# Eight state-space groups per operand set, and four weight pairs open at a feed-forward layer's start, in a hybrid encoder layer

## The chip, the cores and the metric

The kernel runs on one core of one Trainium2 chip. The metric is the time of one execution on the device in microseconds: 2114.1 us as the median of three runs (2113.96 to 2119.34).

## The reference

One encoder layer over 1024 tokens of 1024 channels, in fp32. Cut to what is computed:

```python
h = h + 0.5 * (silu(n1(h) @ Wg1) * (n1(h) @ Wu1)) @ Wd1        # n: RMSNorm, D_FF = 2816
z_ssm, q, k, v, g_ssm, g_att = split(n2(h) @ W_in)             # 512, 3 x 512, 2 x 1024 columns
# 32 groups of 16 channels, 64 complex states each, scanned in both directions
lb = exp(lam * dt);  bb = ((lb - 1) / lam) * B
s_t = lb * s_{t-1} + bb @ u_t;   y = Re(C s)                   # forward + backward, + D * z_ssm
y = gelu(y);  y = y * sigmoid(y @ W_glu + b_glu)
att = neighbourhood_attention(q, k, v)                         # 8 heads, 16 x 64 grid, window 8 x 16
h = h + (sigmoid(g_ssm) * (y @ W_bs) + sigmoid(g_att) * (att @ W_ba)) @ W_out
h = h + 0.5 * (silu(n3(h) @ Wg2) * (n3(h) @ Wu2)) @ Wd2
out = n4(h)
```

## The kernel before, in words

Every large product is made of three TensorE passes: both operands are split into a high part in the short fp32 form (`fp32r`) and the rest, and hi*hi, hi*lo, lo*hi are added up in one PSUM bank. ScalarE (ACT) makes the high part by a CAST, VectorE (DVE) the rest by a subtraction. The weights pass through the class `Weights`: SP loads a raw tile of 512 KB (`wr`, four buffers, `RAWS`), and `fill` splits up to seven units ahead into `wp` tiles.

The feed-forward layers use a scheme of seven products instead of eight for a pair of blocks. A pair f holds a row block of the gate's and one of the up projection's weights; its units q = 1 to 7 take raw quarters of them or sums of quarters (`ws`, four DVE additions per pair in `blocks`), against the matching combinations of activations in `T[q]` (tiles `tq`, split likewise). A unit is 12 matmuls of 128x512. The products of a pair share three PSUM banks, so the order of the units is free within limits: `FIRST` opens two pairs at a layer's begin, q by q; later pairs go one after the other by `THEN`. `gate_up` runs the units, takes t (ACT copy of q = 1), u and v out of PSUM, and after each unit calls `W.fill`, the deferred steps (`poke`), the steps that build further `T[q]` (`rest` in `feed`) and one piece of work put off.

The state-space layer runs in 16 blocks of two groups. Its instructions are issued by a generator, `ssm_steps`, which is advanced every sixth matmul of the gate and value products, so that TensorE goes on with those. Per block: `ssm_prep` forms the operands bb, bi, cc, ci and the padded pad (GpSimd, called POOL, does the products in `bbar`, ACT the copies); `ssm_wide` multiplies them by the tables of powers `pw` and `po` into le and lo (DVE, 128x512); `ssm_operands` makes TensorE matrices of them; `ssm_table` doubles a table of cosines and sines in seven levels, for four groups at a time; `ssm_scan` rotates, scans (four scans of 128x128) and rotates back; `ssm_leave` multiplies out. `ssm_k0`, once for every eight groups, repeats the products of `bbar` on 128x128 tiles. `ssm_params`, earlier, forms the powers and copies them into `pw` and `po` by 16 ACT copies at its end.

`project` is the product with W_out; each d and half ends in an addition to h, and in the sums of squares for the next norm: `acc` is summed over partitions by four small matmuls (ones,acc), `rstd` works on DVE from rtm to `diag`, and four matmuls by `diag` spread the result. The end of the kernel scales by the last norm in spans (`finish`, `leave`). Each engine works in its own order as written; the code's order is the schedule.

Of the kernel before, what the change touches and what calls it, by code (L numbers as in the profile page):

```python
# [43 lines left out]
RAWS, PARTS = 4, 8  # L44


FILLED, ACT, TAIL = 7, 26, 3
NP = NF // 2

FIRST = (1, 2, 6, 7, 5, 4, 3)  # L50
THEN = (1, 6, 2, 7, 5, 4, 3)


class Weights:
# [59 lines left out]
    def blocks(self, p):  # L114
# [12 lines left out]
        st["S"] = {1: a11, 6: s2, 2: a12, 7: s3, 5: a21, 4: a22, 3: s4}  # L127
        st["left"] = {0: {1, 2}, 1: {4, 5}}
# [5 lines left out]
    def prepare_one(self):  # L134
# [16 lines left out]
        else:  # L151
# [4 lines left out]
            else:  # L156
                p, q = u[1:]
                self.blocks(p)
                st = self.pairs[p]
                src = st["S"][q]  # L160
                if q == 6:
                    self.step(4)
# [7 lines left out]
            else:  # L170
                for i, left in st["left"].items():
                    if q in left:
                        left.remove(q)
                        if not left:
                            self.drop(st["raw"] + i)
# [5 lines left out]
        if u[0] == "p":  # L181
            for v in self.units[self.split : self.split + 4]:
                if v[0] == "p" and self.loaded >= self.pairs[v[1]]["raw"] + 2:
                    self.blocks(v[1])

# [23 lines left out]
class Body:  # L209
# [35 lines left out]
    def rstd(self, st, half, then=None, n=HALF, keep=True, at=0):  # L245
# [24 lines left out]
        self.defer(1, spread)  # L270
# [71 lines left out]
    def plan_ffn(self, W, name, wg, wu, wd, plain):  # L342
# [4 lines left out]
        order = [((name, f), q) for q in FIRST for f in fs[:2]] + [((name, f), q) for f in fs[2:] for q in THEN]  # L347
# [25 lines left out]
    def combine(self, x, gcol=None):  # L373
# [34 lines left out]
        g = lambda k: self.vecs[:, gcol + k : gcol + k + 1]  # L408

# [7 lines left out]
        def ahead_scaled(rs):  # L417

            for j in range(4):
                f[2].append(small())  # L420
                m(f[3][j], f[3][j], rs, ALU.mult)
                less(f[2][j], f[3][j], b11[j])
                part(6, j, f[2], 4)
            for j in range(4):
                m(b12[j], b12[j], rs, ALU.mult)
            for j in range(4):
                self.scale(x, j + 4, 1, gcol, rs)

        def diff(o, u, v):
# [10 lines left out]
            "T3": lambda: parts(7, f[3], 4),  # L440
            "t1": lambda: diff(b12, b11, b12),
# [64 lines left out]
    def gate_up(self, plain, after):  # L506
# [5 lines left out]
        order = [(f, q) for q in FIRST for f in fs[:2]] + [(f, q) for f in fs[2:] for q in THEN]  # L512
# [4 lines left out]
        for n, (f, q) in enumerate(order):  # L517
# [31 lines left out]
            elif q == 3:  # L549
# [4 lines left out]
                st[f] = None  # L554
            W.fill(FILLED)
# [37 lines left out]
    def feed_down(self, h, src, done, spans):  # L593
# [70 lines left out]
        for j, sl in enumerate(spans):  # L664
            for i in range(4):
# [5 lines left out]
                work()  # L671
# [3 lines left out]
        work(NF)  # L675


    def ssm_params(self, pool, keep):
# [119 lines left out]
        cmul(lam(5, 4), lam(1, 4), wide(4, 4), 4)  # L798
        yield
# [32 lines left out]

        self.PW, self.PO = (keep.tile([P, 2, NB, 2, 2, 8], F32, name=n) for n in ("pw", "po"))
        for c in (0, 1):
            for i in (0, 1):
                for o, x, y in (
                    (self.PW, L[0:64, c, 0:8, :], L[64:128, c, 7::-1, :]),
                    (self.PO, L[0:64, c, 1:9, :], L[64:128, c, 8:0:-1, :]),
                ):
                    for half, z in ((slice(0, 64), x), (slice(64, 128), y)):  # L840
                        nc.scalar.copy(o[half, c, :, i], z.rearrange("p s (b g) -> p b g s", g=2))
        yield

    def ssm_k0(self, q):
# [3 lines left out]
        bc = pool.tile([P, 8, 64], F32, name="k0bc", bufs=1)  # L848
# [1012 lines left out]
```

## Time and profile before

| what | value |
| --- | --- |
| median of 3 runs | 2114.1 us |
| the profiled execution | 2112.26 us, span 2110.4 us |
| mean granted TensorE clock | 0.982 |
| PE / PE weight load busy | 95% / 77% |
| DVE, ACT, POOL busy | 69%, 40%, 10% |
| DMA | 316.59 MB, 150 GB/s mean |

Times in the trace count from the span's start. The stages, roughly: feed-forward 1 to 700 us, state-space inputs to 735, gates and values with the state-space blocks to 1072, attention, gating and W_out to 1440, feed-forward 2 to the end. Matmuls overlap, so the sum of their durations says little; the steady pace is read from the number of matmuls in a stretch without a wait.

### The profile page before, as it was taken

The numbers are of one execution on the slowest core, as the hardware profiler recorded it, in microseconds if no ns is written. First come the engines' busy times: TensorE is split into PE (matmuls) and PEld (weight loads), VectorE is DVE, ScalarE is ACT, GpSimd is POOL, SyncE is SP. The second block draws the span as 40 slices with busy tenths as digits, with TensorE's granted clock in tenths as the row PEclk, the third lists the DMA queues.
The fourth block names the chain that finished last, engine by engine and source line by source line (L and its number), as shares of the span: only waits on it lengthen the run. The fifth ranks groups of instructions, "written<-read, shape, count | busy, mean of one in ns | idle before, by whom it ended". The sixth has DMA issues, their size and how long they took to land.

```text
span 2110.4 us, 26907 instructions
## 1 busy us (share of the span) xinstructions
PE 2008.1 (95%) x9394; PEld 1633.4 (77%) x9394; DVE 1455.4 (69%) x2711; ACT 834.9 (40%) x1595; POOL 221.1 (10%) x308
## 2 busy tenths in 40 slices
PE   8999999999999799899999999997999999999996
PEld 6778888878888688677877778775788888878885
DVE  6986666656566658898565778668766666657556
ACT  7332233224545324334444573334323222334443
POOL 0011101100000033342000303100001100000000
PEclk9999999999999999999999999999999999999998
DMA  4167666648655143232321333532556665457553
GB/s 175 68 170 188 182 168 175 164 155 279 230 201 189 47 142 98 91 102 89 132 78 43 98 122 123 206 124 76 149 166 181 150 190 155 141 188 273 180 193 120
DMA packets 167879, 316.59 MB, mean 150 GB/s; under 512 B 20288, under 2 KB 40384, under 8 KB 167744
## 3 DMA queue, kind: packets, MB, share of 16 engines
q1 hardware_dynamic: 148608, 288.72, 40.4%
q0 software_dynamic: 12672, 23.07, 7.5%
q10 hardware_dynamic: 6464, 3.08, 0.5%
q8 instruction: 74, 1.21, 0.2%
q14 instruction: 61, 0.50, 0.1%
HBM read 244.88 MB, written 116.10 MB: 171 GB/s over the span
## 4 chain that ended last, share of the span: by engine, by line
PE 69%; DVE 20%; ACT 5%; issue 3%; DMA 2%; ACTq 0%; POOL 0%; SPq 0%; DVEq 0%; POOLq 0%
PE ps L214 68%; DVE tq L301 1%; DVE wp L166 1%; DVE tab L937 1%; DVE wp L146 1%; DVE ww L1026 1%; DVE tb L1012 1%; DVE lt L928 1%; DVE ta L1011 1%; DVE gl L1494 1%; PE ps L1281 1%; ACT wp L145 1%; DVE le L928 1%; DMA h<-in_x 1%; DMA y<-ys 1%
## 5 line engine op out<-in xcount | busy, mean ns | idle before, releaser
L214 PE MATMUL ps<-tq,wp 128*128 128x512 f32 x3444 | 795.1, 392 | 22.1 <-DVE u L515 8.3
L214 PEld LDWEIGHTS ps<-tq,wp 128*128 128x128 f32 x3444 | 648.9, 189 | 167.7 <-DVE tq L301 10.2
L214 PE MATMUL ps<-ap,wp 128*128 128x512 f32 (+1 forms) x1884 | 426.0, 387 | 6.4 <-ACT ap L300 4.0
L214 PEld LDWEIGHTS ps<-ap,wp 128*128 128x128 f32 x1884 | 349.7, 189 | 81.2 <-ACT ap L300 5.2
L214 PE MATMUL ps<-uh,wp 128*128 128x512 f32 x1088 | 327.1, 406 | 17.3 <-ACT wp L145 17.3
L214 PEld LDWEIGHTS ps<-uh,wp 128*128 128x128 f32 x1088 | 206.4, 193 | 65.7 <-ACT wp L145 18.5
L166 DVE TENSOR_TENSOR wp<-wr,wp 128x512 fp32r<-128x512 f32 x318 | 217.5, 685 | 53.3 <-ACT wp L165 53.2
L165 ACT CAST wp<-wr 128x512 fp32r<-128x512 f32 x318 | 191.5, 616 | 61.5 <-PE ps L214 60.1
L214 PE MATMUL ps<-ul,wp 128*128 128x512 f32 x544 | 185.6, 401 | 2.0 <-DVE ul L280 2.0
L545 ACT ACTIVATE v<-v 128x512 f32<-128x512 f32 x41 | 25.9, 632 | 318.0 <-DVE v L515 318.0
L301 DVE TENSOR_TENSOR ap<-ar,ap 128x512 fp32r<-128x512 f32 x154 | 105.8, 688 | 59.6 <-ACT ap L300 59.0
L300 ACT CAST ap<-ar 128x512 fp32r<-128x512 f32 x154 | 95.4, 620 | 114.6 <-DMA ar<-tq 108.1
L146 DVE TENSOR_TENSOR wp<-wr,wp 128x1024 fp32r<-128x1024 f32 (+2 forms) x72 | 85.9, 1197 | 66.3 <-ACT wp L145 65.8
L214 PEld LDWEIGHTS ps<-ul,wp 128*128 128x128 f32 x544 | 103.7, 192 | 25.4 <-DVE ul L280 2.8
L166 DVE TENSOR_TENSOR wp<-ws,wp 128x512 fp32r<-128x512 f32 x123 | 84.1, 685 | 48.7 <-ACT wp L165 48.7
L87 POOL DMA_DIRECT2D sums<-in_wd x44 | 36.7, 925 | 599.7 <-DMA sums<-in_wd 599.7
L214 PE MATMUL ps<-m,wp 128*128 128x512 f32 x384 | 90.6, 397 | 5.2 <-ACT m L300 3.3
L515 DVE TENSOR_TENSOR v<-t,ps 128x512 f32<-128x512 f32 x41 | 28.1, 686 | 93.9 <-PE ps L214 93.9
L626 DVE SCALAR_TENSOR_TENSOR h<-ps,h 128x512 f32<-128x512 f32 (+1 forms) x76 | 48.6, 657 | 63.7 <-PE ps L214 63.7
L214 PEld LDWEIGHTS ps<-m,wp 128*128 128x128 f32 x384 | 73.0, 191 | 22.1 <-ACT m L300 3.7
L165 ACT CAST wp<-ws 128x512 fp32r<-128x512 f32 x123 | 75.2, 615 | 22.2 <-DVE ws L125 22.2
L145 ACT CAST wp<-wr 128x1024 fp32r<-128x1024 f32 (+2 forms) x72 | 71.0, 996 | 1.4 <-issue 1.3
(215 smaller groups left out, 2254.3 us busy)
## 6 DMA issues: line engine op xcount, KB each, us to landing
ar<-tq SPq DMA_DIRECT2D x154, 256.0 KB
wr<-in_wg SPq DMA_DIRECT2D x44, 512.0 KB
wr<-in_wu SPq DMA_DIRECT2D x44, 512.0 KB
sums<-in_wd SPq DMA_DIRECT2D x88, 256.0 KB
wr<-sums SPq DMA_DIRECT2D x88, 256.0 KB
wr<-in_wd SPq DMA_DIRECT2D x66, 256.0 KB
tq<-t SPq DMA_DIRECT2D x61, 256.0 KB
wr<-in_w_in SPq DMA_DIRECT2D x28, 512.0 KB
```

The source lines that it names most:

```text
L87: self.nc.gpsimd.dma_start(out=out, in_=x, accum_op=ALU.add, max_dma_last_dim=2048)
L145: nc.scalar.copy(hi[:, a:b], raw[:, a:b])
L146: nc.vector.tensor_tensor(out=lo[:, a:b], in0=raw[:, a:b], in1=hi[:, a:b].bitcast(F32), op=ALU.subtract)
L165: nc.scalar.copy(hi, src)
L166: nc.vector.tensor_tensor(out=lo, in0=src, in1=hi.bitcast(F32), op=ALU.subtract)
L214: self.nc.tensor.matmul(out, lhsT, rhs, start=start, stop=stop, skip_group_check=go_on)
L300: self.nc.scalar.copy(hi, x)
L301: self.nc.vector.tensor_tensor(out=lo, in0=x, in1=hi.bitcast(F32), op=ALU.subtract)
L515: add = lambda o, u, v: nc.vector.tensor_tensor(out=o, in0=u, in1=v, op=ALU.add)
L545: nc.scalar.activation(out=s["v"], in_=s["v"], func=AF.Silu, scale=-1.0)
L626: nc.vector.scalar_tensor_tensor(out=t, in0=bank[:, sl], scalar=c, in1=t, op0=ALU.mult, op1=ALU.add)
L928: m = lambda o, x, y, op: self.nc.vector.tensor_tensor(out=o, in0=x, in1=y, op=op)
```

## The change

Two things, with small ones beside them. (1) The state-space operands are made for eight groups at once (`ssm_quad`): products on DVE, copies on ACT, only a memset on POOL. The tables of cosines and sines are made for eight groups as well, operands and all that follows come one iteration later (21 iterations instead of 20), le and lo lie in the big pool, and lt shares a buffer with ta. The powers are copied right after they are formed, pw by ACT, po by POOL. (2) `FIRST` becomes a list of 28 units that opens four pairs. Units q = 1 and 2 read the raw tile without waiting for its sums. There are five raw buffers and 24 instead of 26 activation buffers; T2 and the rest are built in smaller steps, later; `project` fills the weights at its end and forms sums early (`early`). The deferred norm of half 1 starts one step earlier. At the start a small activation is put ahead of the loads; at the end ACT scales all spans.

```diff
-RAWS, PARTS = 4, 8
-FILLED, ACT, TAIL = 7, 26, 3
+RAWS, PARTS = 5, 8
+FILLED, ACT, TAIL = 7, 24, 3
-FIRST = (1, 2, 6, 7, 5, 4, 3)
+FIRST = tuple((int(x[1]), int(x[0])) for x in "10 11 12 20 21 22 13 60 61 23 70 71 50 51 40 41 30 31 62 72 52 42 32 63 73 53 43 33".split())
+def order_of(fs):
+
+    return [(fs[i], q) for i, q in FIRST] + [(f, q) for f in fs[4:] for q in THEN]
...
             if p not in self.pairs:
-                self.pairs[p] = {"raw": len(self.raws)}
...
+        self.steps.append(lambda: self.done(p, "sums"))
+        st["S"] = {6: s2, 7: s3, 5: a21, 4: a22, 3: s4}
+    def done(self, p, q):
+
+        st = self.pairs[p]
+        for i, left in st["left"].items():
+            if q in left:
+                left.remove(q)
+                if not left:
+                    self.drop(st["raw"] + i)
...
-                self.blocks(p)
-                st = self.pairs[p]
-                src = st["S"][q]
-                if q == 6:
-                    self.step(4)
+                if q < 3:
+                    i = self.pairs[p]["raw"]
+                    self.load(i + 1)
+                    while i not in self.tiles:
+                        self.step()
+                        self.load(i + 1)
+                    src = self.tiles[i][:, hs(q - 1)]
+                else:
+                    self.blocks(p)
+                    src = self.pairs[p]["S"][q]
+                    if q == 6:
+                        self.step(5)
...
+    def early(self, n):
+
+        ps = []
+        for u in self.units[self.split :]:
+            if u[0] != "u" and u[1] not in ps:
+                ps.append(u[1])
+            if len(ps) == 2:
+                break
+        for p in ps:
+            if self.loaded >= self.pairs[p]["raw"] + 2:
+                self.blocks(p)
+        self.step(n)
```
```diff
+            self.poke()
-        rest = {2: ("T3",), 4: ("t1",), 5: ("T1", "t4"), 7: ("T4",), 9: ("B22",)}
+        rest = {4: ("T3",), 5: ("b12",), 6: ("t1",), 7: ("T1",), 8: ("b22",), 9: ("t4",), 10: ("T4",), 12: ("B22",)}
-            self.poke()
...
+        self.PW, self.PO = (keep.tile([P, 2, NB, 2, 2, 8], F32, name=n) for n in ("pw", "po"))
+        for c in (0, 1):
+            for i in (0, 1):
+                for copy, o, x, y in (
+                    (nc.scalar.copy, self.PW, L[0:64, c, 0:8, :], L[64:128, c, 7::-1, :]),
+                    (nc.gpsimd.tensor_copy, self.PO, L[0:64, c, 1:9, :], L[64:128, c, 8:0:-1, :]),
+                ):
+                    for half, z in ((slice(0, 64), x), (slice(64, 128), y)):
+                        copy(o[half, c, :, i], z.rearrange("p s (b g) -> p b g s", g=2))
...
-        self.PW, self.PO = (keep.tile([P, 2, NB, 2, 2, 8], F32, name=n) for n in ("pw", "po"))
...
```
```diff
+        bs, cs = (pool.tile([P, 4, 3, 2, 16], F32, tag=n, name=n, bufs=2) for n in ("bs", "cs"))
+        pad = pool.tile([P, 4, 2, 2, 2, 16], F32, name="pad", bufs=2)
+        t = pool.tile([P, 4, 2, 16], F32, name="bt", bufs=1)
+        m = lambda o, x, y, op: nc.vector.tensor_tensor(out=o, in0=x, in1=y, op=op)
+        blocks = lambda x: x.rearrange("p (b g) k -> p b g k", g=2)
+        fr, fi = (blocks(self.f[:, c, gs].unsqueeze(2).to_broadcast([P, 8, 16])) for c in (0, 1))
+        br, bi, cr, ci = (blocks(bc[:, :, 16 * i : 16 * i + 16]) for i in range(4))
+        nc.gpsimd.memset(pad, 0.0)
+        for o, x, y, op in ((bs[:, :, 1], br, bi, ALU.subtract), (bs[:, :, 2], bi, br, ALU.add)):
+            m(o, x, fr, ALU.mult)
+            m(t, y, fi, ALU.mult)
+            m(o, o, t, op)
+        for o, x, sign in ((bs[:, :, 0], bs[:, :, 2], -1.0), (cs[:, :, 0], cr, 1.0), (cs[:, :, 1], ci, -1.0), (cs[:, :, 2], cr, -1.0)):
+            nc.scalar.activation(out=o, in_=x, func=AF.Copy, scale=sign)
+        for d in (0, 1):
+            s = slice(64 * d, 64 * d + 64)
+            for c in (0, 1):
+                nc.scalar.copy(pad[s, :, c, :, d, :], bs[s, :, 1 + c])
+        flat = pool.tile([P, 2, 4, 32], F32, name="flat", bufs=1)
+        for c in (0, 1):
+            nc.scalar.copy(flat[:, c], bs[:, :, 1 + c].rearrange("p b g k -> p b (g k)"))
+        self.quads[q] = (bs, cs, pad)
...
```
```diff
-        if b % 2 == 0:
-            tab = self.tab = pool.tile([P, 2, 4, P], F32, tag="tab", name="tab", bufs=1)
+        if b % 4 == 0:
+            tab = self.tab = pool.tile([P, 2, 8, P], F32, tag="tab", name="tab", bufs=1)
+            gs = slice(2 * b, 2 * b + 8)
-                sh = [P, 2, 4, n]
+                sh = [P, 2, 8, n]
-                y = pool.tile([P, 2, 4, 64], F32, tag="tb", name="ty", bufs=1)[:, :, :, 0:n]
-                m(new, old, self.cosines[:, i, g4].unsqueeze(1).unsqueeze(3).to_broadcast(sh), ALU.mult)
-                m(y, old[:, ::-1], self.sines[:, i, :, g4].unsqueeze(3).to_broadcast(sh), ALU.mult)
+                y = pool.tile([P, 2, 8, 64], F32, tag="ty", name="ty", bufs=1)[:, :, :, 0:n]
+                m(new, old, self.cosines[:, i, gs].unsqueeze(1).unsqueeze(3).to_broadcast(sh), ALU.mult)
+                m(y, old[:, ::-1], self.sines[:, i, :, gs].unsqueeze(3).to_broadcast(sh), ALU.mult)
                 m(new, new, y, ALU.add)
...
```
```diff
-        self.load_bc(0)
-        k0 = [self.ssm_k0(q) for q in range(4)]
-        next(k0[0])
-        for n in range(NB + 4):
+        for n in range(NB + 5):
             if 0 <= n - 3 < NB:
-                self.ssm_enter(n - 3)
+                self.ssm_loads(n - 3)
+            if 0 <= n - 4 < NB:
+                self.ssm_enter(n - 4)
             yield
-            scan = self.ssm_scan(n - 3) if 0 <= n - 3 < NB else iter(())
-            if 0 <= n - 4 < NB:
-                self.ssm_leave(n - 4)
+            if 0 <= n - 5 < NB:
+                self.ssm_leave(n - 5)
-            if 0 <= n - 1 < NB:
-                self.ssm_operands(n - 1)
-            if n == 1 or (n % 4 == 0 and 0 < n < NB):
-                next(k0[n // 4])
+            if 0 <= n - 2 < NB:
+                self.ssm_operands(n - 2)
+            if n == 1:
+                next(quad[0])
+            if n % 2 and n // 4 < 3:
+                next(quad[n // 4 + 1])
             yield
-            if n < NB:
-                self.ssm_prep(n)
-                self.ssm_table(n - 2)
+            if 0 <= n - 3 < NB:
+                self.ssm_table(n - 3)
+            if n == 0 or (n % 4 == 2 and n // 4 < 3):
+                next(quad[(n + 2) // 4])
...
```
```diff
+            else:
+
+                W.prepare(W.at + 3)
...
+                if half and d == KD - 1:
+                    W.fill(PARTS)
+                if half and d > 3:
+                    W.early(3)
...
+            self.eps = const.tile([P, 1], F32, name="eps")
+            nc.vector.memset(self.eps, EPS)
+
+            nc.scalar.activation(out=const.tile([P, 1], F32, name="none"), in_=self.eps, func=AF.Square)
...
@@ -1660,8 +1684,8 @@
-                steps["T2"]()
-                self.feed(steps, 3, {0: lambda: self.evac_plain(*held.pop(0)), 3: lambda: self.evac_plain(*held.pop(0))})
+                evac = lambda: self.evac_plain(*held.pop(0))
+                self.feed(steps, 3, {0: evac, 1: steps["T2"], 3: evac})
...
-                        self.defer(2, lambda: self.rstd(sums[half], half, (first, second)[half], HALF, False))
+                        self.defer(2 - half, lambda: self.rstd(sums[half], half, (first, second)[half], HALF, False, 0, 1 + half))
```
```diff
-                        if at == last:
-                            nc.vector.scalar_tensor_tensor(
-                                out=t, in0=t, scalar=self.vecs[:, GF + k : GF + k + 1], in1=rs[:, :n],
-                                op0=ALU.mult, op1=ALU.mult,
-                            )
-                        else:
-                            nc.vector.tensor_tensor(out=t, in0=t, in1=rs[:, :n], op=ALU.mult)
+                        nc.vector.tensor_tensor(out=t, in0=t, in1=rs[:, :n], op=ALU.mult)
-                        if at:
+                        if at == last:
                             leave(k)
                         else:
                             self.todo.append(lambda k=k: leave(k))
-                            if i < last:
-                                tt = h[d][half][:, spans[i][1]]
-                                nc.scalar.activation(out=tt, in_=tt, func=AF.Copy, scale=self.vecs[:, GF + d : GF + d + 1])
+                            tt = h[d][half][:, spans[i][1]]
+                            nc.scalar.activation(out=tt, in_=tt, func=AF.Copy, scale=self.vecs[:, GF + d : GF + d + 1])
...
+                self.work(KD // 2)
+                self.poke()
+                self.poke()
+                self.work(KD)
                 while self.later:
                     self.poke()
```

On ACT, where the state-space inputs are made, this is the order before (wr to wp are weight splits, `sines` and `pw`, `po` belong to `ssm_params`):

```order
L145 CAST wp<-wr 128x1024
L266 COPY rs<-ps 128x512
L831 ACTIVATE sines<-sines 128x32 x7
L841 COPY pw<-lpow 64x16x16 x2
L841 COPY po<-lpow 64x16x16 x2
L841 COPY pw<-lpow 64x16x16 x2
L841 COPY po<-lpow 64x16x16 x2
L841 COPY pw<-lpow 64x16x16 x2
L841 COPY po<-lpow 64x16x16 x2
L841 COPY pw<-lpow 64x16x16 x2
L841 COPY po<-lpow 64x16x16 x2
L145 CAST wp<-wr 128x1024 x3
```

and after:

```order
L159 CAST wp<-wr 128x1024
L849 COPY pw<-lpow 64x16x16 x8
L296 COPY rs<-ps 128x512
L882 ACTIVATE sines<-sines 128x32 x7
L159 CAST wp<-wr 128x1024 x3
L907 ACTIVATE bs<-bs 128x4x32
L907 ACTIVATE cs<-bc 128x4x32 x3
L911 COPY pad<-bs 64x4x2x16 x4
L914 COPY flat<-bs 128x128 x2
L1182 COPY g<-ps 128x512 x2
L159 CAST wp<-wr 128x1024
```

The eight pw copies have moved ahead of `rs` and the sines, the po copies have left ACT, and the three splits follow the sines directly.

On PE behind the last block's products (`sx,lo`), before; `uh`, `ul` against `wp` are the value products, and the attention starts behind them:

```order
L214 MATMUL ps<-sx,lo 128x128 x2
L214 MATMUL ps<-wp,uh 128x512 x9
L214 MATMUL ps<-wp,ul 128x512 x4
L214 MATMUL ps<-wp,uh 128x512 x4
L214 MATMUL ps<-wp,ul 128x512 x4
L214 MATMUL ps<-wp,uh 128x512 x12
L214 MATMUL ps<-wp,ul 128x512 x4
L214 MATMUL ps<-wp,uh 128x512 x4
L214 MATMUL ps<-wp,ul 128x512 x4
L214 MATMUL ps<-wp,uh 128x512 x12
L214 MATMUL ps<-wp,ul 128x512 x4
L214 MATMUL ps<-wp,uh 128x512 x4
```

(two more rows of 4 and 8 of them follow), and after:

```order
L244 MATMUL ps<-sx,lo 128x128 x2
L244 MATMUL ps<-wp,ul 128x512 x3
L244 MATMUL ps<-wp,uh 128x512 x12
L244 MATMUL ps<-wp,ul 128x512 x4
L244 MATMUL ps<-wp,uh 128x512 x4
L244 MATMUL ps<-wp,ul 128x512 x4
L244 MATMUL ps<-wp,uh 128x512 x8
L244 MATMUL ps<-uh,wp 128x512 x2
```

77 value matmuls stood behind the last block, and 35 stand there now.

On DVE at the end of W_out, before, behind the last row block's `tf` (L125 forms the sums of weights, L166 the lower parts, L239 begins the norm):

```order
L125 TENSOR_TENSOR ws<-wr 128x512
L166 TENSOR_TENSOR wp<-wr,wp 128x512 x2
L125 TENSOR_TENSOR ws<-ws,wr 128x512
L125 TENSOR_TENSOR wr<-wr 128x512
L125 TENSOR_TENSOR ws<-wr,ws 128x512
L125 TENSOR_TENSOR ws<-wr 128x512
L166 TENSOR_TENSOR wp<-ws,wp 128x512
L125 TENSOR_TENSOR ws<-ws,wr 128x512
L125 TENSOR_TENSOR wr<-wr 128x512
L125 TENSOR_TENSOR ws<-wr,ws 128x512
L166 TENSOR_TENSOR wp<-ws,wp 128x512 x3
L239 TENSOR_SCALAR rtm<-ps 128x8
```

and after, from the splits ahead of the last addition to h (L1571) on:

```order
L187 TENSOR_TENSOR wp<-wr,wp 128x512 x5
L1571 TENSOR_TENSOR h_11695<-h_11695,ps 128x512
L263 TENSOR_TENSOR acc<-acc,sq 128x512
L444 SCALAR_TENSOR_TENSOR tf<-h_11695,vecs,tf 128x512
L269 TENSOR_SCALAR rtm<-ps 128x8
L270 RECIPROCAL rt<-rtt 128x8
L271 TENSOR_TENSOR rtt<-rt 128x8
L272 SCALAR_TENSOR_TENSOR rtt<-rtt,rtm 128x8
L273 SCALAR_TENSOR_TENSOR rt<-rtt,rt 128x8
L286 TENSOR_SCALAR diag<-ident,rt 128x128 x4
```

Fourteen sums and splits have left the place between the last `tf` and the norm; five splits in a row, and three sums ahead of them, now stand before the last addition to h.

## Rows read from the trace of the kernel before

**Rows 1.** Stretches: start:end, length, busy by engine (instructions), clock, DMA share, GB/s.
```profile
50.00:100.00 50.00, 45.09 (x187) 36.42 (x186) 49.01 (x80) 19.04 (x35) 0.00 (x0) 0.94 0.20 74
100.00:150.00 50.00, 45.17 (x191) 34.92 (x190) 40.56 (x67) 19.14 (x34) 4.24 (x5) 1.00 0.52 146
700.00:740.00 40.00, 29.44 (x123) 23.91 (x122) 26.67 (x113) 14.50 (x27) 0.00 (x0) 0.87 0.27 67
845.60:971.60 126.00, 113.89 (x601) 94.04 (x600) 109.24 (x246) 48.36 (x126) 49.10 (x88) 0.96 0.30 93
1400.00:1450.00 50.00, 42.69 (x178) 33.20 (x176) 40.00 (x68) 21.23 (x35) 0.00 (x0) 0.97 0.27 92
1450.00:1510.00 60.00, 48.94 (x190) 36.44 (x191) 50.84 (x83) 23.71 (x41) 5.03 (x6) 0.94 0.44 124
1600.00:1650.00 50.00, 50.00 (x223) 41.40 (x222) 33.76 (x54) 15.40 (x28) 6.03 (x8) 1.00 0.61 162
```
**Rows 2.** PE's waits by line and releaser: us in total, times, longest.
```profile
PE ps L214 <- ACT wp L145: 18.9, 4, 10.6
PE ps L214 <- POOL bt L878: 8.8, 7, 1.5
PE ps L214 <- DVE u L515: 8.3, 4, 2.7
PE ps L214 <- DVE diag L256: 7.4, 4, 4.4
PE ps L960 <- DVE le L928: 7.3, 5, 2.0
PE ps L214 <- ACT qk L1214: 4.4, 1, 4.4
```
**Rows 3.** Time lines of PE and of SP's queue, start of feed-forward 1.
```profile
80.98 5.38 PE L214 MATMUL ps<-tq,wp 128*128 128x512 f32 x23
91.60 0.33 SPq L105 DMA_DIRECT2D wr<-in_wg  x1
```
**Rows 4.** Time line of ACT at the state-space inputs: start, us, instruction, count.
```profile
720.64 1.27 ACT L841 COPY pw<-lpow 64x256 f32<-64x256 f32 x2
...
730.75 2.94 ACT L145 CAST wp<-wr 128x1024 fp32r<-128x1024 f32 x3
```
**Rows 5.** DVE groups, 845.6 to 971.6 us: busy us, mean ns, idle before.
```profile
L1026 DVE TENSOR_TENSOR_SCAN ww<-rho,ww 128x128 f32<-128x128 f32 x32 | 12.4, 447 | 0.0
L937 DVE TENSOR_TENSOR tab<-tab,ty 128x8 f32<-128x8 f32 (+6 forms) x28 | 8.7, 312 | 1.0
L937 DVE TENSOR_TENSOR tab<-tab,cosines 128x8 f32<-128x8 f32 (+6 forms) x28 | 8.7, 311 | 1.0
L146 DVE TENSOR_TENSOR wp<-wr,wp 128x1024 fp32r<-128x1024 f32 x7 | 8.7, 1240 | 5.2 <-ACT wp L145 5.2
L937 DVE TENSOR_TENSOR ty<-tab,sines 128x8 f32<-128x8 f32 (+6 forms) x28 | 8.5, 304 | 0.0
L928 DVE TENSOR_TENSOR lt<-pw,bi 128x512 f32<-128x512 f32 x8 | 5.5, 687 | 8.3 <-ACT bi L907 8.3
```
**Rows 6.** Time line of PE in a block: small products and the next.
```profile
858.55 0.61 PE L214 MATMUL ps<-sx,lo 128*128 128x128 f32 x4
859.00 0.39 PE L214 MATMUL ps<-su,sm 128*128 128x128 f32 x2
```
**Rows 7.** DVE, same stretch, one form of the table apart.
```profile
L937 DVE TENSOR_TENSOR tab<-tab,ty 128x128 f32<-128x128 f32 x4 | 1.2, 292 | 0.1
```
**Rows 8.** Time line of DVE: four scans beside POOL's k0 products, and without.
```profile
916.10 2.10 DVE L1026 TENSOR_TENSOR_SCAN ww<-rho,ww 128x128 f32<-128x128 f32 x4
930.71 1.36 DVE L1026 TENSOR_TENSOR_SCAN ww<-rho,ww 128x128 f32<-128x128 f32 x4
```
**Rows 9.** Time lines of ACT's first instruction and of DVE's leaves in the last span but one.
```profile
4.15 1.28 ACT L279 ACT_TABLE_LOAD   x1 [4.15 <-DMA h<-in_x]
2094.03 2.77 DVE L1754 TENSOR_TENSOR h<-h,rs 128x256 f32<-128x256 f32 x8
```

More of the change, by code (lines that the diff above doesn't have):

```diff
@@ L79, in plan_pairs @@
             if p not in self.pairs:
-                self.pairs[p] = {"raw": len(self.raws)}
+                self.pairs[p] = {"raw": len(self.raws), "left": {0: {1, 2, "sums"}, 1: {4, 5}}}
                 self.raws.extend(pairs[p])
@@ L170, in prepare_one @@
             else:
[L171 to L175, printed above, removed]
+                self.done(p, q)
         if self.split in self.jobs:
@@ L182, in prepare_one @@
             for v in self.units[self.split : self.split + 4]:
-                if v[0] == "p" and self.loaded >= self.pairs[v[1]]["raw"] + 2:
+                if v[0] == "p" and v[2] > 2 and self.loaded >= self.pairs[v[1]]["raw"] + 2:
                     self.blocks(v[1])
+    def early(self, n):
[9 more added lines that the diff above has]
+        self.step(n)
     def cost(self, i):
@@ L243, in rsqrt, with rstd @@
         nc.vector.scalar_tensor_tensor(out=y, in0=t, scalar=1.5, in1=y, op0=ALU.add, op1=ALU.mult)
-    def rstd(self, st, half, then=None, n=HALF, keep=True, at=0):
+    def rstd(self, st, half, then=None, n=HALF, keep=True, at=0, wait=1):
         nc = self.nc
@@ L268, in spread @@
                 then(self.rs[half] if keep else ps)
-        self.defer(1, spread)
+        self.defer(wait, spread)
     def enter(self, h, k, half, gcol, u, pool, tag):
@@ L346, in plan_ffn @@
         fs = range(plain, NF)
-        order = [((name, f), q) for q in FIRST for f in fs[:2]] + [((name, f), q) for f in fs[2:] for q in THEN]
+        order = [((name, f), q) for f, q in order_of(fs)]
         sums = self.sums[name]
@@ L417, in ahead_scaled, with second @@
         def ahead_scaled(rs):
[L419 to L427, printed above, removed]
+            for j in range(5):
+                if j < 4:
+                    f[2].append(small())
+                    m(f[3][j], f[3][j], rs, ALU.mult)
+                    less(f[2][j], f[3][j], b11[j])
+                if j:
+                    part(6, j - 1, f[2], 4)
+            scales.append(rs)
+        def second(rows):
+            for rs in scales:
+                for j in range(4):
+                    if rows:
+                        self.scale(x, j + 4, 1, gcol, rs)
+                    else:
+                        m(b12[j], b12[j], rs, ALU.mult)
         def diff(o, u, v):
@@ L511, in gate_up @@
         fs = range(plain, NF)
-        order = [(f, q) for q in FIRST for f in fs[:2]] + [(f, q) for f in fs[2:] for q in THEN]
+        order = order_of(fs)
         st = {f: {} for f in fs}
@@ L923, in ssm_wide @@
+        st["le"] = place("le")
+        st["lo"] = place("lo")
         for o, w, x, y in ((st["le"], self.PW, bb, bi), (st["lo"], self.PO, cc, ci)):
[L924 removed]
+            t = pool.tile([P, 2, 2, 8, 16], F32, tag="ta", name="lt", bufs=1)
             f = lambda v: v.rearrange("p c g s k -> p (c g) s k")
```

97 lines of the change are left out of this document (20 added, 77 removed).

## The prediction

> **What bounds the kernel now.** The stretches of the trace come first, because a mean over the whole span mixes stages. In a steady feed-forward stretch TensorE (PE) has 223 matmuls in 50 us, no wait and full clock, so 0.224 us is the price of a 128x512 matmul (1600 to 1650) [rows 1]. VectorE (DVE) and ScalarE (ACT) are busy for 34 and 15 of those 50 us. The change alters neither the number of large matmuls nor their kind, so time can only come from stretches with fewer of them. There are four: 378 where 446 would fit (50 to 150), 123 where 179 would (700 to 740), 368 where 491 would (1400 to 1510), and the state-space blocks. Counted as matmuls of 0.224 us that is 15.2, 12.5 and 27.6 us. The waits by releaser then say on whom PE waits there: one ACT split for 10.6 us, POOL's bt and DVE's le in the blocks for 16.1, u and diag at the feed-forward begins, qk once for 4.4 [rows 2]. The clock falls beside such waits (0.94, 0.87, 0.94 in rows 1), which is why the counts lose more than the waits' sum.
>
> **Feed-forward 1, the begin.** Four pairs open instead of two, so q = 6 and later come further behind their sums. But PE reaches units faster than weights come. The first unit starts at 80.98 and a unit lasts 12 x 0.224 = 2.7 us, so the fifth, 21, is due at 91.7. The seventh, 13, needs the seventh raw tile, and with five buffers it can be asked for only when the sums of pairs 0 and 1 are done; before, SP asks for a tile of this layer at 91.60 [rows 3]. 512 KB at the 146 GB/s of the stretch from 100 to 150 are 3.6 us (an estimate), so ACT, which splits ahead in order, stands at 13's CAST until about 95, and is through with it and the next copy, 0.6 us each, some 2 us later. Behind that CAST on ACT is the copy of t for the next pair, which frees the bank for 21: I expect PE to wait there for about 5.7 us. Against that the waits for u, some others and most of the reduced clock go: of 15.2 lost I let 11.7 remain. Term: +3.5. Bounds: +10 if the raw comes in time, -2 if the clock falls beside the longer pause as it does now (0.94 from 50 to 100).
>
> **State-space inputs.** ACT works from 720.64 on 16 copies of powers and starts the next weight split at 730.75; PE waits for that split 10.6 us [rows 2, 4]. After, the pw copies stand ahead of the sines, beside matmuls that are already fed, and the po copies are on POOL, which is idle there (0.00 busy in the stretch). The split then follows the last of the sines at about 720.7. A gap of about 1 us stays, since the split and its lower part take 1.0 and 1.2 us. Of 12.5 lost 11.5 return. Bounds 9 to 12.5; if the cover of the copies is gone, they cost eight times 0.63 us, still half of before.
>
> **State-space blocks.** Between 845.6 and 971.6 there are 32 scans, so eight iterations of 15.75 us, in which DVE is busy for 109.24 / 8 = 13.65 and idle for 2.1; half of that, 8.3 / 8 = 1.04, is lt waiting for ACT's bi, which waits for POOL [rows 1 and 5]. DVE with its waits sets the period. An iteration is seven steps, one at every sixth large matmul: 42 of the 601 / 8 = 75 matmuls are large and 33 small. The next small product starts 0.45 us after four of them (858.55 to 859.00), 0.112 each [rows 6], so PE needs 9.4 + 3.7 = 13.1 us. Per iteration the change:
> - takes the wait for bi away (operands are there an iteration ahead): -1.04;
> - doubles the tables. Now one costs (8.7 + 8.7 + 8.5) / 4 = 6.5 us per two iterations [rows 5]. For eight groups every level is twice as wide: the smallest level (3 x 0.17) goes and one of 128x1024 comes, 3 x 1.24 by the split of that size. 9.7 us per four iterations against 13: -0.8;
> - adds six products of 128x128 per four iterations to DVE, 0.29 each [rows 7]: +0.45;
> - takes POOL's products away from beside DVE. Four scans take 1.36 us alone and 2.10 beside POOL's k0 products [rows 8]; all 32 took 12.4 instead of 10.9: -0.2;
> - adds lt's wait for ta's buffer, which ACT's copies of the scan free: the nearest row is the split's wait for ACT, 5.2 / 8; I take a third of it less than what otherwise goes, -0.3 for all small waits.
>
> The sum is 15.75 - 1.9 = 13.85. About 13 iterations have everything, so 24.7 us. A table for eight groups is a burst of 9.7 instead of 6.5 us, with scan and leave behind it in DVE's order; the operands stand an iteration ahead, which hides about half. I take 1.5 us of PE wait for each of three such bursts inside. Term: +20. Lower bound +8: only the wait for bi goes (13.5) and a burst costs the 3.2 us it grew, with some clock. Upper bound +31: the period is PE's 13.1 (13 x 2.65 = 34, less the bursts).
>
> On the fourth item the Trainium skill (SBUF — State Buffer, "SBUF: two separate sides") says that a DVE instruction with two inputs in SBUF and a GpSimd instruction that reads SBUF exclude each other for the whole instruction. The trace shows a lengthening, not a whole wait: 0.74 us on four scans. By the rule DVE could win back up to POOL's busy time, 49.1 / 8 = 6.1 us an iteration, and PE would set the period; that is the rival below.
>
> **Attention's begin.** PE waits 4.4 us for qk [rows 2]. The chain from the last block's leave over gelu and back is the same, but 35 value matmuls instead of 77 stand behind the last `sx,lo`, since the blocks end one iteration later: 42 x 0.224 = 9.4 us less cover. Part returns, as ACT's q copies now go between. Term: -6; bounds -9.4 and 0.
>
> **Feed-forward 2, the begin.** The norm's start, rtm, no longer has 14 sums and splits ahead of it, so most of the 4.4 us for diag goes, and T2 no longer stands in one piece before the first units; u (5.8 of its 8.3 us lie here) has more units to come in [rows 2]. In return three sums and five splits, 8 x 0.6 = 4.8 us, stand before the last addition to h, and ones,acc waits for it: I expect 5.5 us there and about 3 at T4. Of 27.6 lost 13.5 return. Bounds +22 (a rest of 5.5) and +8 (only the 4.4 and half of u's waits).
>
> **Start and end.** ACT's table load (1.28 us) begins only when h has landed at 4.15 [rows 9]; put ahead of it, up to 1.3 return, or nothing if the first weights come later still: +0.6. The Trainium skill (ScalarE: Activation LUTs, "What ACT_TABLE_LOAD costs") counts 2.7 us for a switch, with a drain; by it the term would be up to 2.7. The row has 1.28. At the end the eight products of the last span but one (2.8 us of DVE) are put off until the last sums are through [rows 9]: +2.7, bounds 2 and 4, the upper by the plain product in the last span. The down products (activation buffers 24 for 26): 0, bounds -2 and +1; DMA has 0.61 of its share there, and the loads are issued well ahead.
>
> **Sum.** 3.5 + 11.5 + 20 - 6 + 13.5 + 0.6 + 2.7 = 45.8. The profiled execution took 2112.3 us, 1.8 less than the median; 2112.3 - 45.8 + 1.8 = 2068.
>
> **Rivals.**
> - The openings give nothing: raw tiles come too late at both begins, and the 17 us stay. For: five buffers for eight raws; against: at feed-forward 2 the tiles can be loaded during W_out. 2085.
> - The bursts cost in full: blocks +8, and qk -9.4. For: DVE has 2.1 us of slack per iteration and a burst of 9.7; against: operands an iteration ahead. 2068 + 12 + 3.4 = 2083. With the first: 2100.
> - PE sets the period, as when POOL's products cost DVE more than the scans show: +31 in the blocks, and feed-forward 2 nearer its bound: 2048. Against: DVE would still be busy for 13.1 us.
> - Slower: activation buffers run out at the begins. Four open pairs hold t, u, v, twelve of 24 tiles, where two held six of 26, beside T's own tiles. Then DVE's next sum waits, behind it all splits, until a pair closes; a pair is seven units, 19 us. Twice 19 against 28.8 of gains elsewhere (45.8 - 17): 2123. It decides from 14 us a begin. Against: pairs 0 and 1 close before 2 and 3 take u and v.
> - It doesn't do what it says: another engine sets every stretch, 2114.
>
> **Chances.** Forecast 0.41, openings 0.17, bursts 0.14, both 0.07, PE-bound 0.07, slower 0.08, nothing 0.06. The range 2046 to 2102 leaves out the last two. Within 0.3% (6.3 us, what a measurement here can tell) lies the last, 0.06; slower 0.08; faster 0.86.
>
> **What would show it.** In the changed profile: no wait of more than 2 us for wp at 720 to 735; blocks about 13.9 us apart with no wait for bi, POOL nearly idle; a longer wait for qk; 1400 to 1510 with about 430 large matmuls instead of 368; at 80 to 150 one wait of 5 to 6 us for t. The forecast is wrong if the blocks stay above 15 us, or if waits for activation tiles appear on DVE at the begins.

## The result, and the profile after

The changed kernel takes 2126.45 us as the median of six runs (2126.22 to 2128.23), against 2115.7 us for the kernel before in its six runs: the ratio is 1.0052, with a 95% interval of 1.0041 to 1.0062. The change makes the kernel half a per cent slower; the forecast was 2068 us and the range ended at 2102. The profiled executions lie 15.1 us apart (spans 2110.4 and 2125.5), as that of before (2112.26 us) was faster than each of its six timed runs.

The profile after, PE's waits by line and releaser (us in total, times, longest), in answer to [rows 2]:

```profile
PE ps L244 <- DVE u L555: 19.8, 5, 8.8
PE ps L244 <- ACT wp L159: 12.1, 4, 6.1
PE ps L244 <- DMA su<-zs: 10.6, 2, 7.6
PE ps L244 <- ACT qk L1232: 10.6, 1, 10.6
PE ps L244 <- ACT sx L1056: 9.9, 3, 4.9
PE ps L244 <- DVE acc L263: 8.9, 3, 5.3
PE ps L244 <- ACT t L576: 6.3, 1, 6.3
```

What was to go has gone: bt and le are no releasers any more, diag has 3.4 us left, and the ACT split's longest wait is 6.1 us, at the kernel's start. In their place stand new ones: u rose from 8.3 to 19.8, qk from 4.4 to 10.6, and su and sx are new. All of PE's waits together rose from 95.3 to 107.0. In stretches (busy us and instructions by engine, clock, DMA share, GB/s), in answer to [rows 1]:

```profile
100.00:150.00 50.00, 43.32 (x183) 35.42 (x183) 45.71 (x75) 23.90 (x44) 4.18 (x5) 0.94 0.42 115
700.00:740.00 40.00, 33.23 (x131) 26.24 (x130) 32.47 (x162) 10.11 (x19) 4.99 (x8) 0.92 0.19 41
809.30:1021.00 211.70, 191.25 (x1012) 160.57 (x1013) 167.90 (x338) 80.29 (x154) 1.05 (x2) 0.95 0.28 93
1465.00:1545.00 80.00, 67.91 (x274) 52.77 (x273) 64.33 (x104) 29.07 (x52) 4.13 (x5) 0.91 0.35 96
```

The begins of the two feed-forward layers (first and last row) still run at a granted clock of 0.94 and 0.91. The third row holds 14 iterations of the blocks, from first scan to first scan. DVE is busy for 167.90 / 14 = 12.0 us in each, less than the 13.1 that were forecast, and yet an iteration lasts 15.1 us. In the kernel before the same 14 iterations are

```profile
790.10:1004.40 214.30, 197.31 (x1039) 162.94 (x1038) 186.92 (x424) 84.41 (x213) 75.59 (x132) 0.96 0.30 94
```

15.3 us each, with DVE at 13.35 and PE at 14.1. DVE lost a tenth of its work and the period one per cent.

**The blocks.** The longest wait there, by engines, in the changed kernel (start, us, engine, line, what; the wait in brackets). First DVE: it ends a table for eight groups, then forms the next le and lo, and only then splits a weight. Then SP's queue, then PE:

```profile
927.48 1.23 DVE L954 TENSOR_TENSOR tab<-tab,ty 128x1024 f32<-128x1024 f32 x1
...
932.48 1.22 DVE L160 TENSOR_TENSOR wp<-wr,wp 128x1024 fp32r<-128x1024 f32 x1
933.62 0.69 DVE L1028 TENSOR_TENSOR ta<-ev,tab 128x512 f32<-128x512 f32 x1
```

```profile
933.73 0.33 SPq L110 DMA_DIRECT2D wr<-in_w_v  x1
934.15 0.38 SPq L1001 DMA_DIRECT2D su<-zs  x1
```

```profile
937.68 1.62 PE L244 MATMUL ps<-su,let 128*128 128x128 f32 x6 [7.62 <-DMA su<-zs]
```

The releaser named is a DMA, but it was only issued at 934.15: SP works in order, the weight load ahead of it waits for a raw buffer, and that comes free when DVE is through with the split at 933.7, 14.6 us after the table began. At the other tables PE waits 3.03 (su), 4.51 and 4.87 us (both sx), 20.0 us at the four together.

**The begins of the feed-forward layers.** DVE at the first of them, the three additions to u (L555), and PE's waits:

```profile
139.56 0.68 DVE L555 TENSOR_TENSOR u<-u,ps 128x512 f32<-128x512 f32 x1
143.29 0.68 DVE L555 TENSOR_TENSOR u<-u,ps 128x512 f32<-128x512 f32 x1
147.02 0.68 DVE L555 TENSOR_TENSOR u<-t,ps 128x512 f32<-128x512 f32 x1
```

```profile
98.66 1.65 PE L244 MATMUL ps<-tq,wp 128*128 128x512 f32 x3 [6.30 <-ACT t L576]
147.84 2.47 PE L244 MATMUL ps<-tq,wp 128*128 128x512 f32 x5 [6.68 <-DVE u L555]
166.01 2.40 PE L244 MATMUL ps<-tq,wp 128*128 128x512 f32 x6 [1.88 <-DVE u L555]
```

The first two additions close pairs 0 and 1 (units 30 and 31), and each is followed on DVE by two products, sums for the down layer and weight splits. The third is that of unit 62, ready at 147.7, which unit 72 needs. Counted by the k-th unit of the layer, the changed kernel is 7 us ahead at the 18th unit, and 6 behind after the 26th. In the second layer, counted from its first unit, it makes up 13.9 us until the 18th and loses 14.7 in the next eight (a wait of 8.77 for u).

**The state-space inputs.** ACT, DVE and PE:

```profile
717.45 5.17 ACT L849 COPY pw<-lpow 64x256 f32<-64x256 f32 x8 [22.61 <-DVE lpow L733]
722.65 0.59 ACT L296 COPY rs<-ps 128x512 f32<-128x512 f32 x1
731.16 0.23 ACT L882 ACTIVATE sines<-sines 128x32 f32<-128x32 f32 x1 [7.93 <-DVE sines L739]
```

```profile
723.27 3.16 DVE L1142 TENSOR_TENSOR z<-ps,rs 128x512 f32<-128x512 f32 x3 [3.22 <-ACT rs L296]
```

```profile
720.11 0.79 PE L244 MATMUL ps<-uh,wp 128*128 128x512 f32 x1 [3.44 <-DVE z L1142]
735.71 0.73 PE L244 MATMUL ps<-uh,wp 128*128 128x512 f32 x2 [3.33 <-ACT wp L159]
```

The eight copies now hold up rs, rs holds up z on DVE, z the sines, and the split that follows the last of these starts at 734.63, not at 720.7. The copies could not start earlier: ACT stood idle for 22.61 us until DVE had powers to copy. DVE's chain that forms them begins late, for it waits for its parameters (sraw). SP's queue, then DVE:

```profile
686.25 10.97 SPq L110 DMA_DIRECT2D wr<-in_w_in  x3
697.32 0.38 SPq L723 DMA_DIRECT2D sraw<-in_ssm_p  x1
```

```profile
700.51 0.18 DVE L741 TENSOR_SCALAR sp<-sraw 128x32 f32<-128x32 f32 x1 [3.64 <-DMA sraw<-in_ssm_p]
```

The early third weight split has brought a third weight load in front of sraw. That load went out only at 696.90, when DVE was through with the split and a raw buffer came free, and sraw behind it. In the kernel before SP issues sraw at 681.79, and DVE begins on it at 689.63 without a wait.

**Attention's begin**, in answer to the 4.4 us of [rows 2]:

```profile
1091.15 1.31 PE L244 MATMUL ps<-qk 64*128 64x256 f32 x6 [10.59 <-ACT qk L1232]
```

### The profile page after: what moved, and what is told of

Read it like the earlier page. It is cut to its first block, busy times and chain, and to the rows that moved or that the text cites. A ratio compares the mean times of both kernels' runs of the same rounds, so it can differ in the third digit from the quotient of the medians.

```text
span 2125.5 us, 26603 instructions
## 1 busy us (share of the span) xinstructions
PE 2012.1 (95%) x9394; PEld 1642.3 (77%) x9394; DVE 1446.1 (68%) x2643; ACT 834.7 (39%) x1540; POOL 134.3 (6%) x144
## 4 chain that ended last, share of the span: by engine, by line
PE 71%; DVE 18%; ACT 4%; DMA 3%; issue 3%; SPq 0%; ACTq 0%; DVEq 0%
PE ps L244 71%; DVE tq L331 1%; DVE tab L954 1%; DVE wp L187 1%; DVE wp L160 1%; ACT wp L159 1%; DVE gl L1512 1%; PE ps L1299 1%; DMA h<-in_x 1%; DVE ty L954 1%; DMA y<-ys 0%; DVE ww L1043 0%; DVE ws L130 0%; DVE u L555 0%; DVE ta L1028 0%
## 5 line engine op out<-in xcount | busy, mean ns | idle before, releaser
L244 PE MATMUL ps<-tq,wp 128*128 128x512 f32 x3444 | 795.8, 393 | 26.9 <-DVE u L555 19.8
L555 DVE TENSOR_TENSOR v<-t,ps 128x512 f32<-128x512 f32 x41 | 28.2, 687 | 83.3 <-PE ps L244 83.3
```

Source lines behind the costliest of these rows:

```text
L244: self.nc.tensor.matmul(out, lhsT, rhs, start=start, stop=stop, skip_group_check=go_on)
L555: add = lambda o, u, v: nc.vector.tensor_tensor(out=o, in0=u, in1=v, op=ALU.add)
```

## The experiments

Differences in us are ratios to the kernel before, times its 2115.7; the changed kernel is at +11.0. The block stage is counted from PE's first gate product to its wait for qk: 340.2 us in the kernel before, 344.8 in the changed one.

**e1, the state-space part alone, and e2, the rest alone.** The diff in two: `ssm_params` to `ssm_inputs` in e1, all else in e2; for e1, against the changed kernel, among others

```diff
-RAWS, PARTS = 5, 8
-FILLED, ACT, TAIL = 7, 24, 3
+RAWS, PARTS = 4, 8
+FILLED, ACT, TAIL = 7, 26, 3
-        order = order_of(fs)
+        order = [(f, q) for q in FIRST for f in fs[:2]] + [(f, q) for f in fs[2:] for q in THEN]
```

and the reverse in e2.

> The kernel before with the state-space part of the change alone (powers copied when formed, operands and tables for eight groups, 21 iterations, early third weight split); all feed-forward, norm, start and end edits are left out. Theory, parts are independent: from the two traces the inputs gain 2.2 us, the blocks lose 4.6, the wait for qk loses 6.2, attention 0.9, so about 9.5 us slower than before, near 2125. Rival, the state-space part is good and only meets late weights of the feed-forward part: 20 us faster than before, near 2095.

> The kernel before with everything but the state-space part: four open pairs, five raw buffers, 24 activation buffers, later T steps, early sums, norm, start and end edits. Theory, independent parts: feed-forward 1 loses 6.3 us, the begin of feed-forward 2 loses 0.8, its down products 1.9, the end gains 3.2: 5.8 us slower, near 2121. Rival, the late state-space part disturbs the second feed-forward layer: no slower than before, 2112 to 2115.

Measured: 2122.86 us, ratio 1.0025 (1.0014 to 1.0037), and 2120.83, ratio 1.0022 (1.0012 to 1.0032). Each part by itself makes the kernel slower, e1 by less than expected, and 5.3 + 4.7 is about the 11.0 of both: within the intervals the parts add. The wait for sraw stands in e1's trace (3.8 us) and not in e2's.

**e3, the closings apart.**

```diff
-... 50 51 40 41 30 31 62 72 52 42 32 63 73 53 43 33
+... 50 51 40 41 30 62 31 72 52 63 42 73 32 53 43 33
```

> The changed kernel with another order of the same 28 units: 62 stands between the closing units 30 and 31, and 63, 73 between 52, 42 and 32, so that no two pairs close back to back ahead of a unit that needs its u. Theory, DVE's backlog of two closings delays u of pair 2: the waits of 6.7 and 8.8 us for u fall below 3 each and the trailing ones of 1.9 go, so 10 to 15 us less than the changed kernel, 2111 to 2116. Rival, weights or activation buffers come late there: the waits move with the units and the time stays at 2126.

Measured: 2111.41, ratio 0.998 (0.997 to 0.999), 15.2 us less than the changed kernel. All waits for u together:

```profile
PE ps L244 <- DVE u L555: 5.5, 3, 2.5
```

against 19.8. Buffers, loads and the number of open pairs are the same, so these waits were DVE's backlog behind two closings. The wait for t at unit 21 is not among them (7.32 here).

**e4, su loaded earlier.** The load moves from the begin of an iteration to behind the previous iteration's leave:

```diff
-        nc.sync.dma_start(out=st["u"], in_=self.zs[b])      # in ssm_loads(n - 3)
                 self.ssm_leave(n - 5)
+            if 0 <= n - 2 < NB:
+                self.ssm_loads_u(n - 2)
```

> The changed kernel with the load of su issued by SP an iteration earlier (behind the previous block's leave), so that it does not stand behind a weight load that waits for DVE. Theory SP queue: the waits for su of 3.0 and 7.6 us go and nothing takes their place, 9 to 11 us less, near 2116. Rival DVE burst: behind the 9.7 us of the table the scan and its copies are as late, PE waits there instead, 0 to 4 us less, 2122 to 2126.

Measured: 2125.61, ratio 1.0051 (1.0031 to 1.0071): no gain. No wait for su is left, and at the same table PE now has

```profile
940.35 1.22 PE L244 MATMUL ps<-sx,lo 128*128 128x128 f32 x4 [6.52 <-ACT sx L1059]
```

in place of 7.62 us for su, and 5.96 in place of 4.51 at the table before. So the place of su's load did not set the time: with it gone, sx, which waits for the scan behind the same DVE work, comes as late.

**e5, the pause ended earlier.** The blocks' generator pauses while the first gates run; it now ends 42 matmuls, one iteration, sooner:

```diff
-PACE, LEAD = 6, (40, 110)
+PACE, LEAD = 6, (40, 68)
```

> The changed kernel with the pause of the block generator ending 42 value and gate matmuls earlier, so that 77 value matmuls stand behind the last block again. Theory cover: the wait for qk falls from 10.6 us to about 4.4 and the rest stays, 5 to 7 us less than the changed kernel, near 2120. Rival, the blocks then meet their operands and powers too early: waits of about the same size appear at the first blocks, 2126.

Measured: 2107.07, ratio 0.996 (0.9947 to 0.9973), 19.5 us less than the changed kernel, three times what was expected. The wait for qk fell by 7.5 us to

```profile
1074.57 1.31 PE L244 MATMUL ps<-qk 64*128 64x256 f32 x6 [3.04 <-ACT qk L1232]
```

and the block stage from 344.8 to 331.7 us; the waits for sx are now 9.3 us in all, none above 2.8, and those for su nearly gone.

**e6, even tables, and e7, tables of four.** e7 takes back the size alone; e6 has the same work as e7 in two pieces:

```diff
-        if b % 4 == 0:
-            tab = self.tab = pool.tile([P, 2, 8, P], F32, tag="tab", name="tab", bufs=1)
+        if b % 2 == 0:                                       # e7: bufs=1, all 7 levels here
+            tab = self.tab = pool.tile([P, 2, 4, P], F32, tag="tab", name="tab", bufs=1)
+        if b % 2 == 0:                                       # e6: bufs=2
+            levels(self.tab, 2 * b, range(5, 7))
+        elif b + 1 < NB:
+            self.start_table()
+            levels(self.next_tab, 2 * b + 2, range(5))
```

> The changed kernel with tables for four groups again, but built in two pieces, five levels in one iteration and two in the next, in two buffers, so that each iteration has about 3.2 us of table instead of none or 9.7. Theory burst: the waits for sx and su at every fourth block (3.0, 4.5, 7.6, 4.9) and the lower clock beside them go, 15 to 25 us less than the changed kernel, 2102 to 2111. Rival, DVE's total in a block sets the time: the table costs 0.8 us more per block, no gain, 2126 to 2135.

> The changed kernel with tables for four groups in one piece, as in the kernel before; operands for eight groups stay. Theory burst: 6.5 us every second block instead of 9.7 every fourth, each below or near the slack, so the long waits shrink below 2 us each, 8 to 15 us less, 2111 to 2118. Rival, DVE's total sets the time: 0.8 us more per block, 10 us more, 2136.

Measured: e6 2120.58, ratio 1.0024 (1.0012 to 1.0036); e7 2137.01, ratio 1.0109 (1.0092 to 1.0126). e7 lost 12.1 us against the changed kernel, about as its rival had it (DVE's total, 13 x 0.8); e6 gained 5.9, between its two expectations. With equal work, e6 is 18.0 us faster than e7: evenness is worth time. How much of the 18 and the 12 it is stays open, because another wait moved too. In e7, where the values' first half ends, ACT's copies of V stand behind the sx of a block with a table ahead of it:

```profile
1032.24 2.08 PE L244 MATMUL ps<-su,let 128*128 128x128 f32 x8 [9.26 <-ACT V L1204]
```

In e6 PE waits 4.78 us there, in the changed kernel 0.72. Nor is the growth of a table from 6.5 to 9.7 us the whole cause: e7's tables are those of the kernel before, and its block stage lasts 352.8 us against 340.2, with 27.8 us of waits. The rest of the change makes the stage longer by itself.

**e8, unit 13 later.**

```diff
-10 11 12 20 21 22 13 60 61 23 70 71 ...
+10 11 12 20 21 22 60 61 13 70 71 23 ...
```

> The changed kernel with unit 13, the first of the fourth pair, two units later (behind 60 and 61), and 23 behind 70 and 71. Theory: the wait of 6.3 us for t at the begin of feed-forward 1 comes from ACT standing at 13's raw tile ahead of a copy of t; it falls below 3, 3 to 6 us less, 2120 to 2123, and feed-forward 2, whose tiles are loaded before, changes by less than 1. Rival, the wait moves to the next unit that needs a late sum: 2126.

Measured: 2123.44, ratio 1.0042 (1.0027 to 1.0057), about 2 us less, within the intervals. The wait for t is gone, so it did come from ACT standing at 13's raw tile; but the later wait for u in that layer grew from 6.68 to 8.72 us.

**e9 and e10, together.** e9 is e3 and e5 in one, e10 adds e6; no other edit.

> The changed kernel with both the order of e3 and the earlier end of the pause of e5. Theory, the two lie in different stages and add: 15 and 19 us less than the changed kernel, 2090 to 2095, about 1% faster than the kernel before. Rival, one of them only shifts a wait that the other meets: 2103 to 2110.

> As e9, with the tables in two even pieces as in e6. Theory burst: the 9.9 us of waits at four blocks that e5 kept mostly go, against 3 us more of table in all hidden: 4 to 8 us less than e9, 2085 to 2090. Rival, DVE's total in a block: no less than e9, 2092 to 2100.

Measured: e9 2091.45, ratio 0.9887 (0.987 to 0.9904); e10 2087.23, ratio 0.9867 (0.9852 to 0.9882). e3 and e5 add: 15.2 and 19.5 against 34.9 for both. The even tables give 4 more, which the intervals don't set apart; the block stage fell from 331.6 to 325.3 us, of which 8.2 are waits.

**e11, the earlier end in the kernel before, and e12, an end only 18 matmuls earlier in the changed one.**

```diff
-PACE, LEAD = 6, (40, 110)
+PACE, LEAD = 6, (40, 68)     # e11, in the kernel before
+PACE, LEAD = 6, (40, 92)     # e12, in the changed kernel
```

> The kernel before, with nothing of the change, its pause ended 42 matmuls earlier. Theory cover: its wait for qk of 4.4 us goes as 119 matmuls stand behind the last block, its blocks are set by DVE as now, 3 to 6 us less than before, 2108 to 2112. Rival, the earlier end itself speeds the blocks (another place of the weight splits among them) and the gain of e5 is nothing of the change's: 15 us less, near 2099.

> The changed kernel with the pause ended 18 instead of 42 matmuls earlier. Theory cover and nothing else: wait for qk 10.6 - 4 = 6.6 us, and the blocks as in the changed kernel, near 2121. Rival, the place of the weight splits among the steps sets the blocks' waits: the block stage changes by over 5 us either way against the changed kernel, with the waits for su and sx at other sizes than 3.0, 4.5, 7.6, 4.9.

Measured: e11 2128.99, ratio 1.0066 (1.0049 to 1.0082): slower, against both expectations. The wait for qk is gone, but the block stage went from 340.2 to 359.2 us, and the waits of [rows 2] for le rose from 7.3 to

```profile
PE ps L960 <- DVE le L928: 14.0, 7, 5.5
```

So the same edit costs 14 us without the change: e5's gain is not to be had without it. e12: 2117.9, ratio 1.0009 (0.9999 to 1.002). The wait for qk is 7.1 us, as cover has it, but the block stage is 335.9, with waits of 1.7, 2.0, 1.0, 4.4 and 5.6: the stage moved by 9 us, which cover doesn't explain; its rival said over 5.

**e13, the weight split later.** In `gates`, with the pause as it was:

```diff
-            w = W.next()
+            w = W.next(1)
+                if n == 24:
+                    W.prepare(W.at + 2)
```

> The changed kernel with its pause as it is, but the next weight split of the gate products issued 24 matmuls into a unit instead of at its start; nothing else moves. Theory, where the split stands to the tables sets the waits: in the block stage the waits at the tables in the gates (3.0, 4.5, 7.6 us) take other sizes and the stage changes by over 4 us, most likely down to 330 to 340 from 344.8. Rival, the start of the blocks within the stage and not the split's place made e5 and e12 faster: the stage stays within 2 us of 344.8 and the time near 2126.

Measured: 2124.18, ratio 1.0037 (1.0022 to 1.0051); block stage 341.7 us. At the same two tables as in the changed kernel (4.51 and 7.62):

```profile
874.10 2.05 PE L244 MATMUL ps<-su,let 128*128 128x128 f32 x8 [7.74 <-DMA su<-zs]
...
937.35 0.71 PE L244 MATMUL ps<-sx,lo 128*128 128x128 f32 x4 [3.50 <-ACT sx L1056]
```

The long wait has gone to the other table, so the split's place has a part in which table costs most. The sum of the waits stayed (20.9 for 21.8), and the stage moved by 3 us, between the two expectations: inconclusive on the 13 us of e5.

**e14, everything that helped.** e10 with e8's order at the start.

> e10 with unit 13 behind 60 and 61 as in e8. Theory: with the closings apart (e3) nothing takes back the wait for t at the begin of feed-forward 1, so 4 to 7 us less than e10, 2080 to 2083. Rival, DVE meets more sums and closings at once there: as in e8, about 3 us less or nothing, 2084 to 2088.

Measured: 2083.41, ratio 0.9846 (0.9832 to 0.9861), 1.5% faster than the kernel before and the fastest of all, 4.4 us below e10 by the ratios: the lower edge of what its theory expected, and the intervals still touch. PE's busy share from 50 to 100 us is whole:

```profile
50.00:100.00 50.00, 50.00 (x221) 41.08 (x220) 46.93 (x76) 18.22 (x33) 2.62 (x3) 1.00 0.41 123
```

## Why the prediction was wrong

By steps, in the profiled executions (forecast, measured; + is a gain):

| term | forecast | measured | in runs |
| --- | --- | --- | --- |
| start | +0.6 | -0.3 | |
| feed-forward 1, begin | +3.5 | -6.0 | e3, e8 |
| state-space inputs | +11.5 | +2.2 | e1 |
| state-space blocks | +20 | -4.6 | e4 to e7, e13 |
| attention's begin | -6 | -6.2 | e5, e12 |
| feed-forward 2, begin | +13.5 | -0.8 | e3 |
| down products | 0 | -1.9 | |
| end | +2.7 | +3.2 | |

Attention lost another 0.9; the sum is -15.3 of 15.1 measured.

- **The blocks failed most, by 24.6 us, in two terms.** The larger is "1.5 us of PE wait for each of three such bursts": 4.5 us were set for them, and the four tables cost 3.0, 4.5, 7.6 and 4.9, 20.0 in all. An iteration of lead in the operands did not help, as what comes late is in-order work behind the table: the scan (sx), the split, and through SP's queue su. e4 shows the waits for su and sx to have one cause, and e6 against e7 that even pieces of the same work cost less; e7 shows that the size of the piece is not all of it. The rival "the bursts cost in full" named the mechanism at 0.14; its price of 12 us was half of what was measured.
- **"DVE with its waits sets the period"** is the other: 1.9 us less on DVE an iteration were taken as 1.9 us less of time, 24.7 in all. But PE was busy for 14.1 of 15.3 us in an iteration before, and its waits in the whole stage were 16.9 us. Those went, as forecast; the 7.8 beyond them would have had to come from the clock, and that was 0.97 in the stage before and after (0.73 from 930 to 940 us, beside the longest of the new waits). DVE is no longer what sets the period: it now has 33.9 us of idle in 14 iterations in front of the weight split alone, waiting for ACT's CAST:

```profile
L160 DVE TENSOR_TENSOR wp<-wr,wp 128x1024 fp32r<-128x1024 f32 x14 | 17.1, 1224 | 33.9 <-ACT wp L159 33.9
```

- **The openings** do what the forecast said until their 18th unit (+7 and +13.9). Raw tiles cost what was foreseen for them, "about 5.7 us" for t (6.30), and DVE waits for no activation tile at either begin, so the rivals on these fall. "Slower" named 2123, within 4 us of the measured time, by a mechanism that did not occur: that is luck. The step left out is what follows: "u has more units to come in" holds at the opening, while the order ends with two closings in a row, whose work on DVE stands ahead of u of the third pair. e3 takes back 15 us by order alone. The "5.5 us" for ones,acc (5.29) were foreseen.
- **The inputs.** "beside matmuls that are already fed" looked at PE only, and the 11.5 us took the sines to end when they did before ("about 720.7"). Counted from the last down products of feed-forward 1 (675.5 and 681.6), the split starts 55.3 us later before and 53.0 after, so 2.2 us are all that came, less than any bound given. The 10.1 us of copies behind the sines are gone, but the last of the sines comes 7.9 us later by the same count (45.0 before, 52.9 after): DVE waits 3.64 for sraw, z waits 3.22 behind the copies, and two DVE products beside POOL's copies take 0.74 and 0.61 for 0.29, 0.77 us in all; together 7.6. No run took these apart.
- **Attention's begin and the end** came out near their terms (-6.2 for -6, +3.2 for +2.7). That ACT's q copies give part of the cover back was not tested.

Open: why the block stage falls by 9 and 13 us when the pause ends 18 and 42 matmuls earlier. The split's place alone gave 3 (e13). That the last blocks then meet fewer value products, where weight splits follow each other twice as fast, is argued from the order only; no run took this apart. Open with it is why e7's stage is 12.6 us longer than that of the kernel before, with the same tables.

## What to carry to other kernels

Before a saving on one engine is booked as time, add up what the bounding engine waits in that stage: the saving can't return more than that and the clock lost beside it. Making the same work in fewer, larger pieces saves instructions and costs evenness; price the largest piece against everything that stands behind it in order on its engine, and on the queues that wait for its buffers. A load moved forward on a queue that works in order holds up all that is issued behind it, as long as its own buffer is not free. A table of order needs its end read as closely as its begin, and a lead or pause that was right for one pipeline depth is a new choice after the depth changes.

## What the runs showed of the hardware that was not expected

DVE's products slow down beside POOL's copies more than the scans in [rows 8] let expect. The same DVE product of 128x128 in the changed kernel, before and beside the po copies (which run on POOL from 717.64 for 5.28 us):

```profile
717.13 0.29 DVE L733 TENSOR_TENSOR lpow<-sc 128x128 f32<-128x128 f32 x1
717.46 0.95 DVE L733 TENSOR_TENSOR sc<-lpow 128x128 f32<-128x128 f32 x2
718.44 0.61 DVE L733 TENSOR_TENSOR lpow<-sc 128x128 f32<-128x128 f32 x1
```

0.61 for 0.29 us: here the delay is 0.32 us, half of one POOL copy (5.28 / 8 = 0.66), where four scans lost 0.74 together. The Trainium skill (SBUF — State Buffer, "SBUF: two separate sides") states an exclusion for the whole instruction; these two products are nearer to it than the scans were, and do not show it. In the blocks, where POOL has almost nothing left, the scans' mean fell from 447 [rows 5] (440 over the same 14 iterations) to 403 ns:

```profile
L1043 DVE TENSOR_TENSOR_SCAN ww<-rho,ww 128x128 f32<-128x128 f32 x56 | 19.1, 403 | 0.0
```
